# K and Q leave PSUM as one 128-row piece and reach their rows by DMA; their weights are split in the first stage and kept in DRAM

## The chip, the cores and the metric

The kernel runs on one core of a Trainium2 chip. Its time is device microseconds (us) of one execution. The engines are called PE (TensorE, the matrix unit, with PEld for its weight loads), DVE (VectorE), ACT (ScalarE), POOL (GpSimd) and SP (SyncE, which here only issues DMAs). Each takes its instructions in the order of its own queue and waits on semaphores for the others. DMAs are issued from SP's queue and from POOL's.

## The reference

Two layers on x (1024 tokens of width 1024, float32). Layer 0 is a gated mixer and a SwiGLU feed-forward of width 2816. Then K and V are made once from the stream, and layer 1 is a differential attention with its own queries, and a second feed-forward.

```python
kv = rms_norm(x, g) @ w_kv                       # K: 8 heads x 2 maps x 64, V: 8 heads x 128
q = (h @ w_q).reshape(B, S, N_HEADS, 2, HEAD_DIM)
...
s = einsum(q, k) * scale + bias                  # ALiBi bias, causal
p = softmax(s)
a = p[:, :, 0] - lam * p[:, :, 1]                # the two maps of a head
o = rms_norm(a @ v, subln) * (1 - lambda_init)
x = x + o.reshape(B, S, V_WIDTH) @ w_o
x = x + swiglu(rms_norm(x, ffn_norm), w_gu, w_down)
```

## The kernel before

The activations lie transposed: width on the 128 partitions, tokens along the rows, in two halves of 512. Every float32 operand of a product is split into a high part (a cast by ACT) and a low part (the rest, a subtraction by DVE), and three products, high x high, high x low and low x high, replace one. `split` is that pair of instructions.

The stages follow each other: the mixer's projections z and u, its spatial gate and the product with w_out (0 to about 395 us, the entry to the first feed-forward included); the first feed-forward (up to about 982 us, its down product from about 735 us); the projection of V, whose result goes to DRAM (`vscr`); the attention, eight heads (1096 to 1482 us); the second feed-forward and the final norm.

In the mixer, `post_z` and `post_u` take each finished product tile out of PSUM: `post_u` multiplies by a row scale on DVE, applies a gelu on ACT, and multiplies into z on POOL. Behind them `more`, sums of the pieces of w_out and of z, is made by POOL for the output product.

In the attention a generator, `proj_stream`, makes K and Q of the next head while the scores of the present one run. It yields between product steps, and the loop over the blocks of a head calls it, so that PE's projection products fill its waits. A head has four parts: K and Q for each half of the tokens. A part is 24 products into one PSUM tile of 128 rows, and rows 0 to 63 belong to the first of the two maps, rows 64 to 127 to the second. The scores take K and Q as operands of 128 rows in which the map's 64 rows of the high part stand beside 64 rows with the low part (K), or with a second copy (Q). Before, for each map, ACT writes the high part of 64 rows and DVE the low part of the 64 rows into place (L1163 to L1167), and for Q a DMA on POOL's queue copies 64 rows to the other 64 (L1169); in the last head ACT and DVE write those too. `get_w` fetches the weights of a head's K or Q with `Pieces`: a load on SP's queue (L184), a multiplication by the norm's gain on POOL (L201), and a split (L163 on ACT, L164 on DVE).

The order of the instructions on an engine is the order in which a list scheduler places them; at the transitions between stages a few orders are written out by hand (`T.order`). The sums of squares for a norm are `acc` (class `Norm`): ACT squares, POOL adds, and DVE adds the last part; PE then sums over the partitions (`dn<-mean,acc`) and spreads the result over rows (`dn<-ident,nr`). In the down products `cut` is a split operand, and L674 forms differences of weight blocks for an algorithm with fewer products.

## Time and profile before

| | us |
|---|---|
| median of 3 runs | 2207.34 |
| lowest and highest run | 2204.45, 2210.29 |
| the profiled execution's own time | 2203.82 |
| its span, first to last instruction | 2202.1 |

The span is a little shorter than the time of the execution, as the time holds what lies around the first and the last instruction. A row of the trace has the start, the duration, the engine, the line, and what the instruction writes and reads (`out<-in`); a bracket behind it gives the time for which the engine stood idle before it, and the instruction that released it.

### The profile page before, as it was taken

What the parts mean: (1) busy time and instruction counts of PE and PEld (TensorE: products, weight loads), DVE (VectorE), ACT (ScalarE), POOL (GpSimd) and SP (SyncE); (2) the same over time, 40 slices, a digit from 0 to 9 for tenths busy, and PEclk for the clock granted to TensorE, in tenths of its full rate; (3) what the DMA queues carried; (4) which work ended last, traced back from release to release, by engine and by line L of the source; (5) the groups of instructions that cost most, each with busy time, mean ns of one, the idle gap of its engine ahead of it and who ended that gap; (6) DMA issues with size and microseconds to landing.
All of it is one profiled execution on the core that took longest, in us unless ns stands there. A gap on an engine that the chain in (4) does not pass through costs nothing.

```text
span 2202.1 us, 30208 instructions
## 1 busy us (share of the span) xinstructions
PE 2118.6 (96%) x10640; PEld 1771.6 (80%) x10640; DVE 1442.2 (65%) x2541; ACT 1217.1 (55%) x2436; POOL 980.5 (45%) x856
## 2 busy tenths in 40 slices
PE   9999888999999989999999999999799999999998
PEld 7888666888888868878788888887588888888887
DVE  5545997544545576775288898865955454547685
ACT  5323455666666534453277777743467676654463
POOL 5023668675766400244123323205876767560024
PEclk9999999999999999999999999999999999999999
DMA  4131111222223774235423334573123232259412
GB/s 163 58 105 66 40 58 72 98 109 101 106 91 120 244 257 158 77 111 161 117 73 91 87 89 122 187 260 118 63 82 115 101 111 101 96 176 355 132 52 105
DMA packets 111321, 265.85 MB, mean 121 GB/s; under 512 B 10401, under 2 KB 20641, under 8 KB 104257
## 3 DMA queue, kind: packets, MB, share of 16 engines
q1 hardware_dynamic: 93808, 224.98, 29.3%
q0 software_dynamic: 17360, 38.93, 6.3%
q8 instruction: 84, 1.38, 0.3%
q14 instruction: 69, 0.56, 0.1%
HBM read 179.47 MB, written 77.07 MB: 116 GB/s over the span
## 4 chain that ended last, share of the span: by engine, by line
PE 78%; DVE 11%; DMA 4%; POOL 3%; issue 2%; ACT 2%; SPq 0%; DVEq 0%; ACTq 0%; POOLq 0%
PE mm L39 54%; PE d L39 15%; PE sc L39 3%; PE po L39 2%; PE tr L42 2%; DVE cut L646 1%; DVE wg L164 1%; DMA w<-in_w_down 1%; DVE w_lo L164 1%; DVE w_hi L164 1%; DMA a<-ascr 1%; DVE E L1242 1%; PE tr L39 1%; DVE x L160 1%; DVE E L1254 1%
## 5 line engine op out<-in xcount | busy, mean ns | idle before, releaser
L39 PE MATMUL d<-cut 128*128 128x512 f32 (+1 forms) x1788 | 407.7, 388 | 15.7 <-ACT cut L645 9.8
L39 PEld LDWEIGHTS d<-cut 128*128 128x128 f32 x1788 | 332.6, 189 | 88.0 <-ACT cut L645 10.8
L462 DVE TENSOR_TENSOR c<-c,mm 128x256 f32<-128x256 f32 (+1 forms) x300 | 151.2, 506 | 179.5 <-PE mm L39 162.0
L137 POOL TENSOR_TENSOR acc<-acc,sq 128x512 f32<-128x512 f32 (+1 forms) x64 | 92.6, 1449 | 378.3 <-ACT sq L133 376.4
L309 DVE TENSOR_TENSOR wg<-row,wg 128x512 fp32r<-128x512 f32 x180 | 116.7, 658 | 94.6 <-ACT wg L308 90.9
L39 PE MATMUL mm<-hT_hi,w_hi 128*128 128x512 f32 x384 | 155.9, 406 | 0.0
L39 PE MATMUL mm<-hT_hi,w_lo 128*128 128x512 f32 x384 | 151.5, 394 | 0.0
L39 PE MATMUL mm<-hT_lo,w_hi 128*128 128x512 f32 x384 | 150.9, 393 | 0.0
L645 ACT CAST cut<-a 128x512 fp32r<-128x512 f32 x110 | 68.1, 620 | 146.4 <-PE d L39 140.5
L39 PE MATMUL mm<-fine,wg 128*128 128x256 f32 x960 | 138.5, 285 | 4.4 <-DVE c L462 3.5
L39 PEld LDWEIGHTS mm<-fine,wg 128*128 128x128 f32 x960 | 130.5, 191 | 14.0 <-ACT wg L308 3.9
L321 ACT COPY c<-mm 128x512 f32<-128x512 f32 x152 | 88.9, 585 | 91.3 <-PE mm L39 50.8
L646 DVE TENSOR_TENSOR cut<-a,cut 128x512 fp32r<-128x512 f32 x110 | 89.2, 811 | 75.0 <-ACT cut L645 74.9
L308 ACT CAST wg<-S 128x512 fp32r<-128x512 f32 x160 | 99.2, 620 | 50.0 <-PE mm L39 49.3
L331 POOL TENSOR_TENSOR S<-graw 128x512 f32<-128x512 f32 x44 | 59.5, 1352 | 147.6 <-DMA graw<-in_w_gu 147.6
L39 PE MATMUL mm<-T1h,wg 128*128 128x512 f32 x352 | 116.8, 393 | 4.8 <-DVE wg L309 2.3
L39 PE MATMUL mm<-T2h,wg 128*128 128x512 f32 x352 | 118.0, 397 | 1.4 <-ACT wg L308 0.9
L39 PE MATMUL mm<-B22h,wg 128*128 128x512 f32 x352 | 117.5, 396 | 1.0 <-DVE wg L164 0.7
L39 PE MATMUL mm<-B11h,wg 128*128 128x512 f32 x352 | 117.7, 395 | 0.5 <-DVE wg L309 0.5
L39 PE MATMUL mm<-T3h,wg 128*128 128x512 f32 x352 | 118.0, 397 | 0.0
L1246 ACT ACTIVATE E<-E,nm 128x256 f32<-128x256 f32 (+7 forms) x128 | 99.5, 778 | 33.2 <-DVE nm L1242 31.5
L341 POOL TENSOR_TENSOR c<-c,c 128x512 f32<-128x512 f32 x80 | 103.5, 1304 | 31.0 <-DVE c L462 31.0
(287 smaller groups left out, 5784.2 us busy)
## 6 DMA issues: line engine op xcount, KB each, us to landing
graw<-in_w_gu SPq DMA_DIRECT2D x44, 1024.0 KB, 4.9
ascr<-c SPq DMA_DIRECT2D x154, 256.0 KB, 2.0
a<-ascr SPq DMA_DIRECT2D x12, 1280.0 KB, 6.4
a<-ascr SPq DMA_DIRECT2D x18, 768.0 KB, 4.9
xscr<-x SPq DMA_DIRECT2D x48, 256.0 KB, 2.1
w<-in_w_down SPq DMA_DIRECT2D x14, 768.0 KB, 10.6
a0b<-ascr SPq DMA_DIRECT2D x12, 768.0 KB, 5.2
x<-xscr SPq DMA_DIRECT2D x16, 512.0 KB, 12.1
```

Of the source, the lines that this page charges most:

```text
L39: return self._keep(self.engine.matmul(*args, **kw))
L137: return (V if last else G).tensor_tensor(self.acc, self.acc, part, op=ALU.add)
L164: return V.tensor_tensor(lo, src, hi.bitcast(F32), op=ALU.subtract)
L308: A.copy(w[:, 0], src)
L309: T.note(line, name, V.tensor_tensor(w[:, 1], near, w[:, 0].bitcast(F32), op=ALU.subtract))
L321: A.copy(r, src)
L331: T.note(line, ("S1", layer, j, gu), G.tensor_tensor(s1, a21, a22, op=ALU.add))
L341: (G if j else V).tensor_tensor(g, g, u, op=ALU.mult)
L462: V.tensor_tensor(c, c, ps, op=ALU.add)
L645: A.copy(o[:, 0], src)
L646: T.note(line, name + ("lo",), V.tensor_tensor(o[:, 1], src, o[:, 0].bitcast(F32), op=ALU.subtract))
L1246: A.activation(Em[:, :L], Em[:, :L], AF.Exp, scale=-1.0, bias=nm, accum_out=acc)
```

## The change

Four things. (1) A part of K or Q leaves PSUM with one ACT and one DVE instruction of 128x512 into a new tile `both`; four DMAs on POOL's queue bring its halves to their rows, for K 128 KB each and for Q 256 KB each. The last head does the same as the others. (2) The weights of K and Q are multiplied by the gain and split in the first stage: `split_weights` makes 16 pieces, one for each call of `next(ahead)` in `post_z` and `post_u`, and stores high and low part to DRAM (`wscr`). Its tiles come from a pool with one buffer. (3) `get_w` loads the two parts from there, by two DMAs on POOL's queue. (4) The gains are loaded earlier, and the memory for the descriptors of POOL's DMAs is set to 4096 bytes.

```diff
+    wscr = tc.dram_tile([2 * H, P, 2, 1024], F32R, name="wscr")
...
+        prep = pool(front, "pre")
...
+        kvg = col(kv_norm, KD, "kvg")
+        bg = col(b_norm, KD, "bg")
+
+        def split_weights():
+
+            for i in range(2 * H):
+                raw = prep.tile([P, KD, P], F32, name="raw")
+                nc.sync.dma_start(out=raw, in_=(w_k, w_q)[i % 2][i // 2].rearrange("p (k c) -> p k c", c=P))
+                G.tensor_tensor(raw, raw, (kvg, bg)[i % 2].unsqueeze(2).broadcast_to([P, KD, P]), op=ALU.mult)
+                both = prep.tile([P, 2, 1024], F32R, name="both")
+                split(both[:, 0], both[:, 1], raw.rearrange("p k c -> p (k c)"))
+                nc.sync.dma_start(out=wscr[i].bitcast(F32), in_=both.bitcast(F32))
+                yield
+
+        ahead = split_weights()
...
             if cb:
+                next(ahead, None)
                 st6 = sm.tile([P, 2, 6], F32, name="st6")
...
             G.tensor_tensor(z[h][:, :, gs], z[h][:, :, gs], u.rearrange("p (j c) -> p j c", c=P), op=ALU.mult)
+            next(ahead, None)
...
                         q = [qp.tile([P, 2, 512], F32R, name=f"Q{m}") for m in range(2)] if kind else None
+                        both = kp_.tile([P, 2, 512], F32R, name="both")
+                        if kind:
+                            A.activation(both[:, 0], ps, AF.Copy, scale=0.125)
+                            V.scalar_tensor_tensor(both[:, 1], ps, 0.125, both[:, 0].bitcast(F32), ALU.mult, ALU.subtract)
+                        else:
+                            split(both[:, 0], both[:, 1], ps)
                         for m in range(2):
                             own, oth = slice(m * 64, m * 64 + 64), slice(64 - m * 64, 128 - m * 64)
-                            if not kind:
-                                A.copy(K[m][own, hs], ps[own])
-                                V.tensor_tensor(K[m][oth, hs], ps[own], K[m][own, hs].bitcast(F32), op=ALU.subtract)
-                            else:
-                                A.activation(q[m][own, 0], ps[own], AF.Copy, scale=0.125)
-                                V.scalar_tensor_tensor(q[m][own, 1], ps[own], 0.125, q[m][own, 0].bitcast(F32), ALU.mult, ALU.subtract)
-                                if h < H - 1:
-                                    G.dma_start(out=q[m][oth], in_=q[m][own])
+                            for i, to in enumerate((own, oth)):
+                                if kind:
+                                    G.dma_start(out=q[m][to], in_=both[own])
                                 else:
-                                    A.activation(q[m][oth, 0], ps[own], AF.Copy, scale=0.125)
-                                    V.scalar_tensor_tensor(q[m][oth, 1], ps[own], 0.125, q[m][own, 0].bitcast(F32), ALU.mult, ALU.subtract)
+                                    G.dma_start(out=K[m][to, hs], in_=both[own, i])
...
-                    src, g = ((w_k, kvg), (w_q, bg))[kind]
                     with tc.issue_after(marks["spill"]):
-                        weights[h, kind] = piece(src[h], g)
+                        w = [wq_p.tile([P, 1024], F32R, name=n) for n in ("w_hi", "w_lo")]
+                        for i in range(2):
+                            G.dma_start(out=w[i], in_=wscr[2 * h + kind, :, i])
+                        weights[h, kind] = w
...
-    nc = bacc.Bacc("TRN2", target_bir_lowering=False, num_devices=1)
+    nc = bacc.Bacc("TRN2", target_bir_lowering=False, num_devices=1, dynamic_dma_scratch_size=4096)
```

The edits move instructions at places that they don't touch, too. The lines of the changed kernel have other numbers: L164 is the same, L682 is L681 of before, L647 is L646, L675 is L674, L988 is L970 and L1048 is L1029.

The first place is POOL's order at the end of the mixer, where L907 is the new multiplication of a weight by its gain, `z<-z,u` the last multiplication of `post_u`, and `more` a sum for the output product. In the changed kernel:

```order
L988 TENSOR_TENSOR z<-z,u 128x4x128 x2
L907 TENSOR_TENSOR raw<-raw,bg 128x1024
L907 TENSOR_TENSOR raw<-raw,kvg 128x1024
L988 TENSOR_TENSOR z<-z,u 128x4x128
L1048 TENSOR_TENSOR more<-wo_1790 128x512 x4
L988 TENSOR_TENSOR z<-z,u 128x4x128 x2
L907 TENSOR_TENSOR raw<-raw,bg 128x1024
L988 TENSOR_TENSOR z<-z,u 128x4x128
L1048 TENSOR_TENSOR more<-z 128x512 x4
```

The three L907 are new, the last of them stands ahead of the last z; the others stand as before.

The second place is DVE's order between the first feed-forward's last sums (`x<-x,d`) and the projection of V (`vt` is the low part of a tile of V, `w_lo` that of its weights, L146 the first step of the norm behind PE's means). Before:

```order
L197 SCALAR_TENSOR_TENSOR w_lo<-raw,kvg,w_hi 128x512 x4
L681 TENSOR_TENSOR x<-x,d 128x512 x4
L137 TENSOR_TENSOR acc<-acc,sq 128x512
L197 SCALAR_TENSOR_TENSOR w_lo<-raw,kvg,w_hi 128x512 x2
L146 TENSOR_SCALAR nm_8354<-dn 128x4
L164 TENSOR_TENSOR vt<-mm,vt 128x4x128
```

And in the changed kernel:

```order
L682 TENSOR_TENSOR x<-x,d 128x512 x4
L164 TENSOR_TENSOR vt<-mm,vt 128x4x128
L197 SCALAR_TENSOR_TENSOR w_lo<-raw,kvg,w_hi 128x512
L137 TENSOR_TENSOR acc<-acc,sq 128x512
L197 SCALAR_TENSOR_TENSOR w_lo<-raw,kvg,w_hi 128x512 x3
L146 TENSOR_SCALAR nm_8475<-dn 128x4
```

The first `vt` and one `w_lo` moved ahead of `acc`. On ACT the cast of that `vt` now stands ahead of four `w_hi`, before it stood behind two of them; on POOL five loads of K and Q weights stand ahead of the last `acc` addition there.

The third place is DVE's order at the start of the last down product. Before:

```order
L646 TENSOR_TENSOR cut<-a_18709,cut 128x512
L646 TENSOR_TENSOR cut<-w_18707,cut 128x512
L646 TENSOR_TENSOR cut<-a_18709,cut 128x512
L674 TENSOR_TENSOR w_18707<-w_18712,w_18707 128x512 x4
L646 TENSOR_TENSOR cut<-w_18707,cut 128x512
L646 TENSOR_TENSOR cut<-a0b,cut 128x512
```

And in the changed kernel:

```order
L675 TENSOR_TENSOR w_18836<-w_18841,w_18836 128x512 x3
L647 TENSOR_TENSOR cut<-a_18838,cut 128x512
L647 TENSOR_TENSOR cut<-w_18836,cut 128x512
L647 TENSOR_TENSOR cut<-a_18838,cut 128x512
L647 TENSOR_TENSOR cut<-w_18836,cut 128x512
L647 TENSOR_TENSOR cut<-a0b,cut 128x512
```

Three of the differences moved ahead of the cuts. On SP's queue one load of `a0b` (768 KB) that stood ahead of the `w` loads now stands further ahead, between loads of `w2b`.

## Rows read from the trace of the kernel before

**Rows 1.** The page's busy times: engine, us, share of the span, instructions.

```profile
PE 2118.6 (96%) x10640; PEld 1771.6 (80%) x10640; DVE 1442.2 (65%) x2541; ACT 1217.1 (55%) x2436; POOL 980.5 (45%) x856
```

**Rows 2.** Windows of the mixer: stretch, its length, then busy time (instructions) by engine.

```profile
core 0: us, PE busy (x) PEld busy (x) DVE busy (x) ACT busy (x) POOL busy (x), PEclk, DMA share, GB/s
150.00:200.00 50.00, 50.00 (x240) 41.65 (x239) 26.57 (x37) 14.85 (x22) 11.39 (x8) 1.00 0.25 95
200.00:250.00 50.00, 43.50 (x184) 33.65 (x182) 41.43 (x43) 20.83 (x38) 33.51 (x22) 0.97 0.17 63
```

**Rows 3.** Windows of the attention, columns as in rows 2.

```profile
1050.00:1450.00 400.00, 394.09 (x2194) 337.70 (x2193) 320.07 (x858) 259.91 (x686) 106.45 (x114) 1.00 0.40 118
1150.00:1200.00 50.00, 49.49 (x287) 42.67 (x287) 44.75 (x122) 36.97 (x99) 14.83 (x15) 1.00 0.30 85
```

**Rows 4.** PE's waits in six heads, 1120 to 1392 us: in total, times, longest.

```profile
PE tr L42 <- DVE E L1254: 2.6, 6, 0.4
```

**Rows 5.** The timeline around one such wait.

```profile
1164.90 1.89 POOL L201 TENSOR_TENSOR raw<-raw,kvg 128x1024 f32<-128x1024 f32 x1
...
1165.28 1.53 DVE L1253 SCALAR_TENSOR_TENSOR cc<-s,nlam,s 128x1 f32<-128x1 f32 x1
...
1168.01 0.84 PE L42 MATMUL tr<-ident,E 128*128 128x128 f32 x6 [0.42 <-DVE E L1254]
```

**Rows 6.** Groups by shape, 1120 to 1392 us: busy us, mean ns, idle before.

```profile
L164 DVE TENSOR_TENSOR w_lo<-raw,w_hi 128x1024 fp32r<-128x1024 f32 x13 | 16.9, 1301 | 0.0
...
L1164 DVE TENSOR_TENSOR K<-mm,K 64x512 fp32r<-64x512 f32 x24 | 16.5, 689 | 2.1 <-ACT K L1163 1.5
...
L201 POOL TENSOR_TENSOR raw<-raw,bg 128x1024 f32<-128x1024 f32 x6 | 13.5, 2254 | 11.2 <-DMA raw<-in_w_q 11.2
...
L1169 POOL DMA_DIRECT2D Q<-Q x22 | 11.5, 522 | 42.5 <-DVE Q L1167 21.0 <-issue 9.9 <-PE tr L42 8.2
```

**Rows 7.** DMA issues, 1120 to 1392 us: KB each, median us to landing.

```profile
Q<-Q POOLq DMA_DIRECT2D x22, 256.0 KB, 3.2
...
raw<-in_w_q SPq DMA_DIRECT2D x6, 512.0 KB, 3.7
```

**Rows 8.** POOL's timeline early in the mixer.

```profile
34.29 2.65 POOL L137 TENSOR_TENSOR acc<-acc,sq 128x512 f32<-128x512 f32 x2
```

**Rows 9.** The timeline at the end of the mixer.

```profile
217.03 1.29 POOL L970 TENSOR_TENSOR z<-z,u 128x512 f32<-128x512 f32 x1 [0.21 <-ACT u L969]
...
230.40 1.75 DVE L164 TENSOR_TENSOR w_hi<-z,w_hi 128x512 fp32r<-128x512 f32 x1
232.07 0.68 DVE L164 TENSOR_TENSOR w_lo<-wo,w_lo 128x512 fp32r<-128x512 f32 x1
```

**Rows 10.** The timeline ahead of the V projection.

```profile
983.77 0.69 DVE L137 TENSOR_TENSOR acc<-acc,sq 128x512 f32<-128x512 f32 x1 [1.18 <-ACT sq L133]
987.15 0.95 PE L39 MATMUL dn<-mean,acc 128*128 128x1 f32 x8
987.22 1.34 ACT L196 ACTIVATE w_hi<-raw,kvg 128x512 fp32r<-128x512 f32 x2 [3.91 <-DMA raw<-in_w_v]
987.98 1.42 DVE L197 SCALAR_TENSOR_TENSOR w_lo<-raw,kvg,w_hi 128x512 fp32r<-128x512 f32 x2 [3.52 <-ACT w_hi L196]
988.47 0.56 ACT L163 CAST vt<-mm 128x512 fp32r<-128x512 f32 x1
```

**Rows 11.** Windows of 4 us in the mixer's output product, columns as in rows 2.

```profile
236.00:240.00 4.00, 1.22 (x5) 0.79 (x5) 4.00 (x6) 1.34 (x3) 0.88 (x1) 1.00 0.12 47
240.00:244.00 4.00, 3.90 (x10) 2.86 (x11) 4.00 (x5) 2.12 (x4) 2.89 (x2) 0.57 0.56 215
```

**Rows 12.** The timeline at the start of the last down product.

```profile
1977.27 11.00 PE L39 MATMUL d<-cut 128*128 128x512 f32 x47
1977.46 0.94 SPq L600 DMA_DIRECT2D w<-in_w_down  x2
...
1985.88 2.50 DVE L674 TENSOR_TENSOR w<-w,w 128x512 f32<-128x512 f32 x4 [0.90 <-DMA w<-in_w_down]
...
1989.03 3.24 PE L39 MATMUL d<-cut 128*128 128x512 f32 x13 [0.77 <-DVE cut L646]
```

More of the change, by code (lines that the diff above doesn't have):

```diff
@@ L1083, in trunk @@
         wq_p = right(mid, "wqk", 4)
-        kvg = col(kv_norm, KD, "kvg")
-        bg = col(b_norm, KD, "bg")
         with ExitStack() as att:
```

## The prediction

> **What bounds the kernel now.** I read the busy times first, then the windows of the two stages that change, then the waits of TensorE (PE) in them, then single stretches in time order. PE works for 2118.6 us [rows 1] of a span of 2202.1 us, so all its idle time together is 83.5 us, and a change can win only what of that lies where it works. It works in two places. In the first stage PE is busy for 50.00 us of the 50 from 150 to 200, with VectorE (DVE) at 26.6 and GpSimd (POOL) at 11.4; from about 205 us, where the gate's last pieces go into the output product, PE falls to 43.5 of 50 and DVE rises to 41.4 [rows 2]. A filler on DVE or POOL is free before 205 us and is paid for behind it. The other place is the attention (about 1096 to 1482 us). DVE is busy 44.75 us of 50 there, which looks like a bound, but PE is at 49.49, and in the 400 us from 1050 on it stands idle for 400 - 394.09 = 5.9 us in all [rows 3]: PE sets the time.
>
> What PE waits for there is told by its waits: 2.6 us in six heads, each time a transpose behind a DVE instruction [rows 4]. One of the six, step by step: POOL multiplies a K weight by its gain for 1.89 us, beside it DVE's tiny `cc`, 128x1, takes 1.53 us, the E behind it comes late, and PE's transposes start 0.42 us late [rows 5]. Six times 0.42 is the 2.6 us. The reader should see that a job of 1.9 us on an engine off the path costs PE 0.4 us by way of DVE.
>
> **The attention.** Each head loses two weight splits on DVE (1.30 us each) and four of the eight subtractions of 64x512 (0.69 us each), since an instruction on 128 partitions does in one what two on 64 did. That is 2 x 1.30 + 4 x 0.69 = 5.4 us of DVE in a head of 45.3 us (six in the 272 us of that view), and two POOL multiplies of up to 2.25 us [rows 6]. None of it is on PE; PE gets back its waits. The 2.6 us go with the multiply beside `cc`; 5.9 us is all its idle time. I take **-4.0**, in the middle, bounds -2.6 and -5.9.
>
> What is added here stands on POOL's queue: 16 transfers for K and Q in a head in place of four, and four loads of weights. With 0.52 us for an issue [rows 6], 16 more are 8.3 us, against 4.1 us of multiplies. POOL's 14.8 us of 50 are 13.4 in a head [rows 3]; they become about 17.6. The bias and r stand behind the new issues, and PE's scores wait for DVE, which waits for those; both have some 27 us of POOL's idle time in a head. K and Q are read only by the next head's scores, so a landing of 3.2 us [rows 7] is hidden. Price nothing, while issues stay near 0.52 us.
>
> One rule of the notes belongs to the row with `cc`. The Trainium skill ("SBUF — State Buffer", section "SBUF: two separate sides") says that DVE and GpSimd hold a common port pair by an exclusive lock, and that the loser blocks for the whole instruction. The trace agrees in kind: 1.53 us for a 128x1 instruction. By the rule the two multiplies of a head could stop DVE for 4.1 us, 25 us in six heads; but DVE is not the bound, and the sum by PE's waits stays at -4.
>
> **The split moved to the front.** Each of 16 steps is a load on SP (3.7 us, as w_q's now [rows 7]), a POOL multiply (1.9 to 2.25 us), an ACT cast and a DVE subtraction (1.30 us) [rows 6], and a store. The step's tiles have one buffer, so the steps stand one behind another, at 9 to 11 us each: 3.7 + 2.25 + 1.30, about 1.1 for ACT (estimated from DVE's), and 1 to 3 us of waiting in the queues. The first multiply stands in POOL's order among the sums of squares at 34 to 38 us [rows 8]. The sixteenth would then be ready at 38 + 15 x (9 to 11) = 173 to 203 us. All together this is 21 us on DVE and 34 us on POOL over 165 us, in which DVE has 23 of 50 us free and POOL 38 [rows 2], while PE is full; a late post is caught by the four PSUM buffers of the products. So the first fifteen cost nothing. Without this cover, every us that a post is late beyond those buffers would be PE's: rival 2.
>
> The sixteenth cannot come when it is ready: in POOL's order it stands behind the four `more` and before the last z product, which starts at 217.03 us, while DVE sets the time [rows 9]. A multiply there puts z and the next `more` off by 2.25 us, DVE's own share of the step is 1.3 us, and beside a POOL instruction DVE's 128x512 pieces take 1.75 instead of 0.68 us [rows 9], 1.1 us for one. Of these 4.65 us about half falls in DVE's and POOL's gaps: **+2.5**, bounds 0 and 5.
>
> **The junction before the V projection.** DVE's sum of squares `acc` starts at 983.77 us, and PE takes its mean products at 987.15 without a wait [rows 10]. After, DVE's `vt` of the first V tile and one w_lo stand ahead of `acc`. `vt` needs PE's whole first tile, which ends where the mean products begin, then ACT's cast (0.56 us); the w_lo needs an ACT w_hi behind that cast (0.67 us) and takes 0.71 us itself; `acc` takes 0.69 us [rows 10]. So `acc` is there at 987.3 + 0.56 + 0.67 + 0.71 + 0.69 = 989.9 us, and the mean products, whose place on PE is unchanged, wait 2.7 us. With the queues' delays **+3**, bounds 2 and 6. The upper bound has two sources: POOL's last part of the same sum now stands behind five loads of weights, and the clock. Behind a window in which PE worked 1.22 us of 4, the granted clock of the next was 0.57, about the lower of the two levels, 1.2 of 2.4 GHz [rows 11]; at that rate 4 us of work lose 1.7 us.
>
> **The second transition, into the last down product.** DVE's differences of w (2.50 us for four) wait for a load issued at 1977.46 us and start at 1985.88; ahead of them it makes three cuts, and PE runs 47 products from 1977.27 to 1988.27 and waits 0.77 us [rows 12]. After, three of the differences stand ahead of those cuts. PE wants the first of the pairs 12 products before the end of the 47, at 1988.27 - 12 x 0.234 = 1985.5 us; it would be there at 1985.88 + 3 x 0.62 + two cuts at about 0.65 = 1989.0 us. PE waits 3.5 us there and no longer the 0.77: +2.7. If the load lands 2 us earlier, since a load of 768 KB leaves its place ahead of it, +0.7. I take **+2**, bounds 0 and 5.
>
> The products of both FFNs from 238 to 940 and from 1520 to 1950 us keep their order on all engines: zero.
>
> **Sum.** -4 + 2.5 + 3 + 2 = +3.5 us. The profiled execution took 2203.82 us; with 3.5 it is 2207.3. The median of the three runs, 2207.34 us, stands 3.5 above that execution, so on the median it is **2211 us**, 0.16% more.
>
> **The rivals.** (1) Faster: the attention gives back all 5.9 us and the two transitions cost nothing, because the DVE instructions moved ahead find their operands early. 2207.3 - 5.9 = 2201.4 us. That both wait for something which the trace shows late (the first tile's end, the load) speaks against it. To be faster by more than 0.3% (6.6 us, about what a measurement can tell from no change) it needs some of PE's idle time elsewhere too.
>
> (2) Slower, by the front's queues. SP and POOL take their instructions in order: a load that lands late holds the multiply, the multiply holds each z product behind it, and the loads of w_u stand on SP behind the stores. The point that decides is the length of a step: the sixteenth multiply keeps its place as long as a step takes under (217 - 38) / 15 = 11.9 us. At 12.5 us it is ready at 225.5, and the output product slides by 8.5 us: 2211 + 8.5 = 2219.5 us. For it speaks that I could only estimate the waiting; against it, that DMA and POOL are nearly idle there.
>
> (3) Slower, by POOL's queue in the attention. Of its 13.4 us in a head, 4.1 go and 2.1 are the four old issues, so 7.2 us remain; POOL fills a head of 45.3 us when 20 issues take (45.3 - 7.2) / 20 = 1.9 us each. From there each further 0.1 us costs 2 us a head, 14 us in seven heads: 2225 us. A mean of 0.52 us over 22 issues [rows 6] speaks against it. The Trainium skill ("DMA: Bandwidth & Descriptors", section "SWDGE vs HWDGE vs iDMA") is for it: plain transfers belong to SP or ACT, and DVE can lock GpSimd out while it writes descriptors. The 22 issues beside a DVE at 44.75 of 50 us do not show this.
>
> (4) The aim is missed, because PE is full: -2.6 us in the attention, and the transitions cost nothing. 2204.7 us.
>
> **How the numbers follow.** Forecast 0.50, with a range of its own of 2205 to 2217 (the terms at their bounds do not all fall on one side); rival 1 0.13, rival 2 0.15, rival 3 0.07, rival 4 0.15. The range reaches from rival 1 to past rival 2, 2200 to 2222 us; rival 3 and the tails stay out. Slower than 2214 us: rivals 2 and 3 and a quarter of the forecast, 0.34. Faster than 2200.7 us: most of rival 1, 0.10. Within 0.3%: the rest, 0.56.
>
> **What the profile after would show.** Attention: heads shorter by 0.4 to 0.6 us, no wait of a transpose for E, DVE near 39 of 50, issues near 0.52 us. Front: no idle PE before 205 us, and the last multiply near 217. Junction: a wait of PE's mean products for `acc`, some 3 us. Second transition: a wait for a cut, some 3 us. The prediction is wrong if PE idles before 205 us, if POOL fills up in the attention, or if the two waits are absent.

## The result, and the profile after

The changed kernel takes 2225.48 us (median of five runs, 2221.72 to 2233.34), the kernel before on the same chip 2204.45 us. The ratio is 1.0093, interval 1.0077 to 1.0109: 21 us slower, where I had forecast 3.5 us. The profiled execution took 2233.34 us, the longest of the five.

PE has 15 us more of busy time than in [rows 1] for the same 10640 instructions, so a part of the loss is work at a lower clock and not waiting: the mean granted clock of the profiled execution is 0.981, before the change 0.989. DVE and ACT have less, POOL has 132 instructions more. This is the page's row of busy times:

```profile
PE 2133.8 (96%) x10640; PEld 1784.4 (80%) x10640; DVE 1420.1 (64%) x2505; ACT 1190.4 (53%) x2400; POOL 1047.8 (47%) x988
```

Every kernel here gives PE the same number of products. So I read, at the borders of a stage, how much later the product with the same number starts than in the profile of before; what the difference grows by in a stage is that stage's loss. In the changed kernel it is +3.3 us at the end of the mixer (205 to 260 us of before's time), +9.6 at the junction ahead of V (980 to 1020), -5.4 in the heads of the attention (1020 to 1396), +7.4 in the last head (1396 to 1475) and +3.7 at the second transition (1972 to 1995). These five make 18.6 us of the 29.5 by which the two spans (2202.1 and 2231.6 us) differ. The other 11 us lie mostly at 280 to 300 us (+2.4), 700 to 850 us (+2.6) and in the tail, 2150 to 2195 us (+4.8). At the first and the last of these a second profile of the kernel before differs from its first one as well (last section); at 700 to 850 us it does so by only 0.4 us, but e12 below, which has every instruction of the changed kernel in the same order, loses 0.2 us there. The medians are only 21 us apart.

**Attention.** First a window that answers to the second of [rows 3], then six heads of 45.3 us of before's length (columns as in [rows 2]). DVE has 38.24 us of 50 instead of 44.75, POOL 20.88 instead of 14.83, and PE 49.91 instead of 49.49:

```profile
1167.00:1217.00 50.00, 49.91 (x295) 43.75 (x294) 38.24 (x118) 31.02 (x93) 20.88 (x33) 1.00 0.65 164
1135.00:1407.00 272.00, 271.46 (x1587) 237.37 (x1586) 207.31 (x625) 170.50 (x499) 112.46 (x171) 1.00 0.67 168
```

The groups by shape in those six heads show an issue at 0.53 us (0.52 in [rows 6]), and `cc` at 0.22 us on the mean and at most. Before, most took 0.22 us too, but six of them took over 1.5 us, as the one in [rows 5]. Of the six waits of [rows 4] none is left:

```profile
L1189 POOL DMA_DIRECT2D K<-both x48 | 25.2, 533 | 32.6 <-ACT both L163 23.4 <-DVE both L164 7.7 <-issue 1.1
L1187 POOL DMA_DIRECT2D Q<-both x47 | 24.4, 535 | 23.0 <-DVE both L1180 20.4 <-DMA oa<-oscr 1.3 <-DMA w_hi<-wscr 0.9
L1272 DVE SCALAR_TENSOR_TENSOR cc<-s,nlam,s 128x1 f32<-128x1 f32 x49 | 10.7, 218 | 1.1
```

**Junction.** PE's waits from 980 to 1010 us are one row, and [rows 10] had none:

```profile
PE dn L39 <- DVE acc L137: 6.0, 1, 6.0
```

The timeline shows what DVE's `acc` stood behind. SP issues the loads of w_v at 990.75 us. ACT needs the first at 998.73 and has stood idle for 3.09 us for it; DVE's w_lo comes behind it, `acc` behind the w_lo:

```profile
990.75 0.87 SPq L184 DMA_DIRECT2D raw<-in_w_v  x2
...
995.68 0.69 DVE L164 TENSOR_TENSOR vt<-mm,vt 128x512 fp32r<-128x512 f32 x1 [5.37 <-ACT vt L163]
...
998.73 1.33 ACT L196 ACTIVATE w_hi<-raw,kvg 128x512 fp32r<-128x512 f32 x2 [3.09 <-DMA raw<-in_w_v]
999.49 0.75 DVE L197 SCALAR_TENSOR_TENSOR w_lo<-raw,kvg,w_hi 128x512 fp32r<-128x512 f32 x1 [3.12 <-ACT w_hi L196]
1000.16 0.68 DVE L137 TENSOR_TENSOR acc<-acc,sq 128x512 f32<-128x512 f32 x1
```

Why the load is late stands in the table of DMA issues from 985 to 1000 us. Eight loads of the new weights, 4 MB, were put into the same stretch by POOL's queue (from 989.54 us), and w_v takes 9.0 us to land; the loads of w_v ahead of the junction took 4.8 before the change (last line, its table from 975 to 992 us):

```profile
w_hi<-wscr POOLq DMA_DIRECT2D x4, 512.0 KB, 10.4
w_lo<-wscr POOLq DMA_DIRECT2D x4, 512.0 KB, 10.6
...
raw<-in_w_v SPq DMA_DIRECT2D x2, 512.0 KB, 9.0
```

```profile
raw<-in_w_v SPq DMA_DIRECT2D x4, 512.0 KB, 4.8
```

The windows (columns as in [rows 2]) show the other part. PE works 0.02 us of 5, and behind that the granted clock is 0.50, the lower of the two levels, and then 0.67. At those rates 4.01 and 5.00 us of work lose 2.0 and 1.7 us. With the wait of 6.0 that is 9.7, against the 9.6 read at the borders:

```profile
995.00:1000.00 5.00, 0.02 (x1) 0.00 (x0) 1.21 (x2) 1.85 (x3) 1.08 (x2) 0.81 1.07 390
1000.00:1005.00 5.00, 4.01 (x14) 3.56 (x15) 2.99 (x6) 1.40 (x3) 1.04 (x1) 0.50 1.12 416
1005.00:1010.00 5.00, 5.00 (x19) 3.96 (x18) 1.23 (x3) 0.51 (x1) 0.00 (x0) 0.67 1.14 396
```

**Last head.** Two waits from 1400 to 1450 us carry most of the loss; PE's waits there make 5.1 us, and at the same place before the change 1.7:

```profile
PE po L39 <- DVE on L1301: 2.4, 1, 2.4
PE tr L42 <- DVE E L1273: 2.2, 1, 2.2
```

Both go back to a load again. The output product's weights w_o land 13.4 us after their issue. In the same stretch are the last twelve of the last head's sixteen K and Q transfers and the loads of `oa`, the attention's output read back for that product (4 MB). Before the change w_o took 5.2 us (second table, 1395 to 1432 us in each profile):

```profile
oa<-oscr POOLq DMA_DIRECT2D x8, 512.0 KB, 8.1
Q<-both POOLq DMA_DIRECT2D x8, 256.0 KB, 10.8
...
raw<-in_w_o SPq DMA_DIRECT2D x2, 512.0 KB, 13.4
...
K<-both POOLq DMA_DIRECT2D x4, 128.0 KB, 11.0
```

```profile
raw<-in_w_o SPq DMA_DIRECT2D x2, 512.0 KB, 5.2
```

ACT stands for each of the two loads, and what PE wants of ACT and DVE stands in their order behind the casts (timeline of ACT):

```profile
1424.66 1.04 ACT L163 CAST w_hi<-raw 128x1024 fp32r<-128x1024 f32 x1 [3.15 <-DMA raw<-in_w_o]
...
1430.85 1.05 ACT L163 CAST w_hi<-raw 128x1024 fp32r<-128x1024 f32 x1 [3.62 <-DMA raw<-in_w_o]
```

From 1425 to 1440 us the granted clock is below full in three windows of 5 us, where it was 1.00 before the change, and that makes most of the rest:

```profile
1425.00:1430.00 5.00, 2.44 (x11) 2.16 (x11) 3.18 (x8) 2.23 (x6) 0.00 (x0) 0.82 1.26 250
1430.00:1435.00 5.00, 2.83 (x15) 2.52 (x14) 2.70 (x8) 3.02 (x11) 0.00 (x0) 0.84 0.43 147
1435.00:1440.00 5.00, 5.00 (x17) 4.03 (x16) 2.32 (x8) 2.39 (x10) 1.04 (x1) 0.66 0.52 184
```

**Front.** The first, the ninth and the last two multiplies of the split on POOL (timeline). From the first to the sixteenth are 181.6 us, 12.1 a step:

```profile
37.30 1.91 POOL L907 TENSOR_TENSOR raw<-raw,kvg 128x1024 f32<-128x1024 f32 x1
...
129.84 1.90 POOL L907 TENSOR_TENSOR raw<-raw,kvg 128x1024 f32<-128x1024 f32 x1 [8.63 <-DVE vl L164]
...
206.00 1.90 POOL L907 TENSOR_TENSOR raw<-raw,kvg 128x1024 f32<-128x1024 f32 x1 [8.59 <-DMA raw<-in_w_k]
218.86 1.89 POOL L907 TENSOR_TENSOR raw<-raw,bg 128x1024 f32<-128x1024 f32 x1
```

From 35 to 205 us PE does not idle. From 200 to 245 us it works 36.79 us, and before the change 38.50 (windows of the two kernels).

**Second transition.** The row of PE's waits, and DVE's timeline, which answers to [rows 12]: three differences stand ahead of the cuts, behind the load.

```profile
PE d L39 <- DVE cut L647: 2.8, 1, 2.8
```

```profile
2005.81 1.90 DVE L675 TENSOR_TENSOR w<-w,w 128x512 f32<-128x512 f32 x3 [5.91 <-DMA w<-in_w_down]
2007.63 0.68 DVE L647 TENSOR_TENSOR cut<-a,cut 128x512 fp32r<-128x512 f32 x1
```

### The profile page after: what moved, and what is told of

It is laid out like the page before. It is cut to its first block, busy times and chain, and to the rows that moved or that the text cites. A ratio compares the mean times of both kernels' runs of the same rounds, so it can differ in the third digit from the quotient of the medians.

```text
span 2231.6 us, 30438 instructions
## 1 busy us (share of the span) xinstructions
PE 2133.8 (96%) x10640; PEld 1784.4 (80%) x10640; DVE 1420.1 (64%) x2505; ACT 1190.4 (53%) x2400; POOL 1047.8 (47%) x988
## 4 chain that ended last, share of the span: by engine, by line
PE 79%; DVE 10%; DMA 4%; POOL 3%; ACT 2%; issue 2%; SPq 0%; DVEq 0%; ACTq 0%; POOLq 0%
PE mm L39 54%; PE d L39 16%; PE sc L39 3%; PE po L39 3%; PE tr L42 2%; DVE cut L647 1%; DVE wg L164 1%; DMA w<-in_w_down 1%; DVE w_lo L164 1%; DVE w_hi L164 1%; PE tr L39 1%; DMA raw<-in_w_o 1%; DMA a<-ascr 1%; DMA raw<-in_w_v 1%; DVE x L160 1%
## 5 line engine op out<-in xcount | busy, mean ns | idle before, releaser
L39 PE MATMUL d<-cut 128*128 128x512 f32 (+1 forms) x1788 | 409.2, 389 | 18.7 <-ACT cut L646 9.4
L646 ACT CAST cut<-a 128x512 fp32r<-128x512 f32 x110 | 68.2, 620 | 148.4 <-PE d L39 141.8
L647 DVE TENSOR_TENSOR cut<-a,cut 128x512 fp32r<-128x512 f32 x110 | 90.2, 821 | 71.9 <-ACT cut L646 71.8
```

The costliest lines, as they stand in the source:

```text
L39: return self._keep(self.engine.matmul(*args, **kw))
L646: A.copy(o[:, 0], src)
L647: T.note(line, name + ("lo",), V.tensor_tensor(o[:, 1], src, o[:, 0].bitcast(F32), op=ALU.subtract))
```

## The experiments

The table has the ratio to the kernel before on the same chip, and what each profile lost (+) or won at the five places, in us, read as above. e0 is the kernel before, profiled once more: what it loses no change has caused. The column "tail" is 2150 to 2195 us.

| kernel | ratio (95%) | front | junction | attention | last head | 2nd trans. | tail |
|---|---|---|---|---|---|---|---|
| changed | 1.0093 (1.0077, 1.0109) | +3.3 | +9.6 | -5.4 | +7.4 | +3.7 | +4.8 |
| e0 before again | one run | 0.0 | 0.0 | 0.0 | -0.1 | +0.6 | +3.7 |
| e1 K/Q only | 1.0030 (1.0019, 1.0041) | 0.0 | 0.0 | -3.4 | +1.1 | +5.3 | 0.0 |
| e2 weights only | 1.0063 (1.0050, 1.0076) | +3.3 | +8.7 | -4.3 | 0.0 | +3.3 | +3.6 |
| e5 loads later | 1.0083 (1.0068, 1.0098) | +3.3 | +7.5 | -5.4 | +6.0 | +4.1 | +4.8 |
| e9 acc first | 1.0068 (1.0045, 1.0092) | +3.3 | +6.7 | -5.4 | +2.0 | +2.2 | +4.8 |
| e10 loads spread | 1.0042 (1.0024, 1.0059) | +3.3 | 0.0 | -5.3 | +0.3 | +4.1 | +3.6 |
| e4 last head old | 1.0071 (1.0044, 1.0097) | +3.3 | +8.8 | -4.7 | 0.0 | +4.4 | +3.6 |
| e8 eight steps | 1.0065 (1.0041, 1.0088) | -1.1 | +8.6 | -5.3 | +1.9 | +3.6 | +4.7 |
| e12 (no effect) | 1.0075 (1.0060, 1.0090) | +3.3 | +8.5 | -5.4 | +2.3 | +3.8 | +3.6 |
| e15 cut first | 1.0069 (1.0049, 1.0089) | +3.3 | +8.9 | -5.4 | +7.6 | -1.0 | +3.7 |
| e11 three repairs | 1.0008 (0.9996, 1.0019) | -0.6 | 0.0 | -3.6 | 0.0 | +3.4 | +3.6 |
| e16 four repairs | 0.9994 (0.9983, 1.0005) | -0.6 | 0.0 | -3.6 | 0.0 | -1.0 | +4.8 |
| e14 K/Q, one repair | 1.0007 (0.9992, 1.0022) | -1.1 | 0.0 | -2.8 | -0.1 | +4.1 | +4.8 |
| e17 K/Q, two repairs | 0.9980 (0.9969, 0.9992) | -1.1 | 0.0 | -2.8 | 0.0 | -1.0 | +3.6 |

The columns do not add up to a kernel's time. Read in the same way, 280 to 300 us, 700 to 850 us and the entry to the second feed-forward (1490 to 1520 us) differ from profile to profile, the last from -0.6 to +4.6 us: there the changed kernel has +1.0 and e12, in the same order, +3.9. The larger memory for descriptors and the earlier loads of the gains are in every kernel of the table but e0, and no run measures them alone; e17 has both and is not slower.

### The two halves of the change: e1, e2

e1 is the changed kernel with the weights as before, without `split_weights`:

```diff
-                        w = [wq_p.tile([P, 1024], F32R, name=n) for n in ("w_hi", "w_lo")]
-                        for i in range(2):
-                            G.dma_start(out=w[i], in_=wscr[2 * h + kind, :, i])
-                        weights[h, kind] = w
+                        weights[h, kind] = piece(src[h], g)
```

e2 has the new weights and the old copies of K and Q:

```diff
-                        both = kp_.tile([P, 2, 512], F32R, name="both")
...
+                            if not kind:
+                                A.copy(K[m][own, hs], ps[own])
+                                V.tensor_tensor(K[m][oth, hs], ps[own], K[m][own, hs].bitcast(F32), op=ALU.subtract)
```

> The changed kernel with its weights as before (load, multiply and split in the attention, nothing in the first stage): only K and Q leave PSUM in one piece. Theory A (three prices at three places: the split in the first stage 6.6 us, the 4 MB of weight loads at the V projection 9.6 us, the transfers of K and Q in the last head 7 us): the first two are gone, the waits of the transposes for E stay as the multiplies stay, so it ends about 5 us above the kernel before, some 2209 us, and PE idles about 5 us or more around the last head. Theory B (the transfers of K and Q fill POOL's queue and the DMA engines through the whole attention and cost most of the 21 us): about 2220 us. Theory C (the prices come from the moved weights alone): 2200 to 2204 us, and no wait in the last head.

> The changed kernel with K and Q written by ACT and DVE to their rows as before: only the weights are split in the first stage and loaded from DRAM. Theory A: the first stage (+6.6) and the V projection (+9.6) cost as in the changed kernel, the heads shorten by about 0.5 us each, the last head is as before; 2204.5 + 6.6 + 9.6 - 3 = about 2217 us. Theory B: near the kernel before, 2204 to 2208 us. Theory C: the whole loss, 2225 us.

Theory A foresaw 5 us for e1 and 13 us for e2; their medians are 7.5 and 14.4 us above that of the kernel before. It put e1's last head at 7 us, which cost 1.1, and left out the second transition, which cost 5.3. Both halves are slower, and the ratios add up to that of the change (0.30% and 0.63%, against 0.93%). Each wins most of the attention by itself, 3.4 and 4.3 us; together they win 5.4, since PE has hardly any idle time left there to give back (0.5 us in the six heads). Front and junction belong to the weights. The last head's large loss is in neither alone. The second transition is in both, though e1 touches nothing near it: what moves there is the order that the scheduler gives DVE.

### The junction: e5, e9, e10

e5 lets the loads of the weights start later, e9 sets DVE's `acc` ahead of the `vt` and the w_lo, e10 spreads the loads of heads 0 and 1 over the tiles of V.

e5, in `get_w`:

```diff
-                    with tc.issue_after(marks["spill"]):
+                    with tc.issue_after(marks["pow"]):
```

e9, in the projection of V:

```diff
+                T.order({0: line["acc", 0, 0, 3] + line["vt", 0, 0]}, [0])
+                T.order({0: line["acc", 0, 0, 3] + line["down", 0, 1, "mean"] + line["vlo", 5]}, [0])
```

e10, in `get_w`, where `marks["vt", ...]` is the store of a V tile:

```diff
-                    with tc.issue_after(marks["spill"]):
+                    with tc.issue_after(marks["vt", h, (2, 5)[kind]] if h < 2 else marks["spill"]):
```

> The changed kernel with the first eight loads of weights from DRAM issued behind the norm ahead of the V projection; DVE's order there falls back to that of before by itself. Theory A (the loads of V's weights landed late, behind 4 MB of other loads, and DVE's sum of squares stood behind one of them): PE's wait of 6.0 us for that sum goes, and the granted clock does not fall there; 9 us less than the changed kernel, about 2216 us. Rival (the sum is late because it stands behind the first V tile on DVE, and the loads do not matter): the same here, as the order changes too, so this run tells only whether the junction carries 9 us; the next one tells which.

> The changed kernel with its eight loads where they are, but on DVE the sum of squares stands ahead of the first V tile, and it and the first step of the norm stand ahead of the four low parts of V's weights that the late loads feed. Theory A1 (the late loads cost only through DVE's order): PE's wait of 6.0 us goes, as with the later loads, about 2216 us, although the loads of V's weights still take 8 us. Theory A2 (PE itself needs what is late, or POOL's five loads ahead of its part of the sum hold it up): the wait moves to another place between 995 and 1010 us and 5 us or more stay, about 2222 us.

> The changed kernel with the first four pairs of weight loads spread over the projection of V, one pair behind the stores of tiles 2, 5, 10 and 13; DVE's order at the junction falls back to that of before. Theory A2 (4 MB at once is what costs, and the wait moves to what lands late wherever they are put together): no wait over 1 us from 985 to 1100 us, 9 us less than the changed kernel, about 2216 us. Rival (the loads themselves, wherever they are, hold up V's stores and PE): PE waits again for the low parts of V's tiles, 2 us or more at each pair.

In e5 and e9 the wait for `acc` is gone, and another stands there, so the 9 us that e5 was to win did not come. e5, PE's waits from 980 to 1035 us: `acc` is first again and w_v lands in 4.4 us, but now the stores of V stand in the same heap of transfers. ACT stands idle for 12.35 us for one of them before it casts the next V tile, and PE waits behind that:

```profile
PE mm L39 <- DVE vt L164: 5.7, 1, 5.7
```

e9, DVE's timeline: `acc` is there at 990.85 us, but the norm's eight multiplications of x start behind the last late w_lo, at 1000.39, and the `vt` that PE waits for (3.9 us) comes at 1007.58:

```profile
990.85 0.69 DVE L137 TENSOR_TENSOR acc<-acc,sq 128x512 f32<-128x512 f32 x1 [3.52 <-POOL acc L137]
...
1000.39 4.86 DVE L810 TENSOR_TENSOR x<-x,dn 128x512 f32<-128x512 f32 x8
...
1007.58 0.68 DVE L164 TENSOR_TENSOR vt<-mm,vt 128x512 fp32r<-128x512 f32 x1
```

In e10 nothing waits there; w_v lands in 4.3 us, and the order that I had priced does not occur: DVE makes `acc` first. The kernel is at 2214.92 us, as theory A2 had it (2216):

```profile
989.37 0.69 DVE L137 TENSOR_TENSOR acc<-acc,sq 128x512 f32<-128x512 f32 x1 [0.83 <-ACT sq L133]
993.71 1.42 DVE L197 SCALAR_TENSOR_TENSOR w_lo<-raw,kvg,w_hi 128x512 fp32r<-128x512 f32 x2 [3.65 <-ACT w_hi L196]
```

So the 4 MB in one place are the cause: with them three different orders lose 9.6 (changed), 7.5 (e5) and 6.7 us (e9), and without them the order of before loses nothing. Since e10 changed both, what the new order alone would have cost is not measured. In the changed kernel 3.09 us of the wait of 6.0 are ACT's standing for w_v; the other 2.9 would be the order's, an estimate from these two rows.

### The last head: e4

e4 gives the last head alone its copies by ACT and DVE back.

```diff
+                        if h == H - 1:
+                            for m in range(2):
+                                own, oth = slice(m * 64, m * 64 + 64), slice(64 - m * 64, 128 - m * 64)
+                                if not kind:
+                                    A.copy(K[m][own, hs], ps[own])
...
+                        else:
                             both = kp_.tile([P, 2, 512], F32R, name="both")
```

> The changed kernel with K and Q of the last head alone written by ACT and DVE as before. Theory A (the transfers of K and Q meet the 4 MB of oa loads, and the load of w_o, which ACT waits for, lands after 13 us instead of 5): the load lands after 5 to 6 us, the 7.4 us in the last head go, about 2218 us. Rival (the 4 MB of oa loads and the w_o load meet badly by themselves, as the heads are shorter): the load still takes over 10 us, 2223 us or more.

The loss there is 0.0, and w_o lands in 4.6 us (DMA issues, 1395 to 1432 us):

```profile
oa<-oscr POOLq DMA_DIRECT2D x4, 512.0 KB, 8.8
...
raw<-in_w_o SPq DMA_DIRECT2D x2, 512.0 KB, 4.6
```

So theory A holds at the place. The ratio, 1.0071, is below the changed kernel's 1.0093 but not clear of the 1.0075 that the same kernel has as e12.

In the kernels whose last head has its K and Q by DMA, w_o's median landing goes with the loss: 9.6 us and +0.3 (e10), 10.5 and +1.1 (e1), 10.5 and +1.9 (e8), 10.8 and +2.0 (e9), 11.1 and +2.3 (e12), 12.5 and +6.0 (e5), 13.4 and +7.4 (changed), 13.6 and +7.6 (e15). e12 and the changed kernel issue the same instructions in the same order, so with nothing else changed the last head costs 2.3 or 7.4 us as the transfers happen to meet.

### The front: e8

e8 makes eight of the sixteen pieces; heads 4 to 7 read the weights of heads 0 to 3.

```diff
-            for i in range(2 * H):
+            for i in range(H):
...
-                            G.dma_start(out=w[i], in_=wscr[2 * h + kind, :, i])
+                            G.dma_start(out=w[i], in_=wscr[(2 * h + kind) % H, :, i])
```

> The changed kernel with eight of the sixteen steps of the split in the first stage; heads 4 to 7 read the weights of heads 0 to 3. Theory A (only the last step, at 218 us, costs): the 6.6 us that PE has lost by 300 us are gone but for what the clock does there, 0 to 4 us stay; 2219 to 2222 us. Rival (the steps cost by their number): half, 3.3 us, stay and about 2222 us. Where between the two readings overlap, the waits of PE from 205 to 300 us decide: with A no step's instruction stands there.

The last multiply is at 116.23 us, and the front wins 1.1 us where it had lost 3.3, so the rival (half of the loss stays) is out. With twelve steps (e11, e16) the loss is gone too: it is that of the last four, whose multiplies stand from 182.21 to 218.86 us. Whether they cost by coming late or by their place in POOL's order, no run separates.

### The second transition: e12, e15

The added order sets the three cuts on DVE ahead of the differences. In e12, and in e11 and e14, the line stood behind its loop and changed no order; e12 is the changed kernel measured a second time.

```diff
                         s = V.tensor_tensor(to[i], x[i], y[i], op=ALU.subtract)
                         T.order({0: [line[name + ("lo",)][2 * i + 1], s.ins]}, [0])
+                        if layer and name[2] == 0 and i < 4:
+                            T.order({0: [line[name + ("lo",)][8], s.ins]}, [0])
```

> The changed kernel with one thing alone: in the second transition DVE makes the cut that PE waits for ahead of the first difference of w, as before the change. Theory A (the order of DVE's instructions is the cause there): PE's wait for that cut goes from 2.8 us to under 1, the difference to the kernel before at that place from +3.7 to under +1, all else as in the changed kernel; time 2222 us, ratio 1.0080. Rival B (the load that the differences wait for is what is late): PE's wait stays at 2 to 3 us, now for the differences, and the time stays at the changed kernel's 2225 us.

> The changed kernel with one thing alone, now in force: in the second transition DVE makes three cuts ahead of the first four differences of w, as before the change. Theory A: PE's wait for a cut falls from 2.8 us to under 1, the difference to the kernel before at that place from +3.7 to under +1; ratio 0.0013 under that of the changed kernel (1.0093 and, in a second measurement, 1.0075), so 1.0062 to 1.008. Rival B: the wait stays at 2 us or more for a cut behind the differences, the ratio where it was.

In e15 PE waits for nothing there, and instead of 3.7 us lost the place wins 1.0: theory A, the order. The ratio, 1.0069, is in A's range, but not clear of e12's 1.0075; the place decides. DVE's timeline has the three cuts ahead of the four differences:

```profile
2002.04 0.88 DVE L647 TENSOR_TENSOR cut<-a,cut 128x512 fp32r<-128x512 f32 x1 [3.89 <-ACT cut L646]
2002.84 0.68 DVE L647 TENSOR_TENSOR cut<-w,cut 128x512 fp32r<-128x512 f32 x1
2003.44 0.68 DVE L647 TENSOR_TENSOR cut<-a,cut 128x512 fp32r<-128x512 f32 x1
2004.04 2.48 DVE L675 TENSOR_TENSOR w<-w,w 128x512 f32<-128x512 f32 x4
```

### All repaired: e11, e16, e14, e17

e11 is e10 with e4's last head and only twelve steps in the front (heads 6 and 7 take their weights as before the change); e16 adds the order of e15. e14 is e1 with e4's last head; e17 adds the order. Beside the edits above, e11 and e16 have:

```diff
-            for i in range(2 * H):
+            for i in range(2 * H - 4):
...
+                if H - 2 <= h < H and (h, kind) not in weights:
+                    src, g = ((w_k, kvg), (w_q, bg))[kind]
```

> Four repairs of the changed kernel together: the loads of heads 0 and 1 are spread over the V tiles, the last head's K and Q are copied by ACT and DVE as before the change, only twelve of the sixteen weights are split in the first stage (heads 6 and 7 get theirs in the attention, as before the change), and DVE makes its cut ahead of the differences of w in the second transition. Theory A (four losses, each with a cause of its own and each removed by its own repair; the attention's gain stays): PE's differences to the kernel before are about 0 at 205 to 260 us, 0 at 980 to 1020, -4.5 in the attention, 0 in the last head, +0.5 at the second transition; time 0.2% under the kernel before, 2199 to 2202 us if that is at 2204.5. Rival B (what one place wins, another gives back, by transfers that land together or by the clock): one of the four places keeps 3 us or more, or a new one appears, and the time is no better than with spread loads alone, ratio 1.004, 2213 us. Rival C (time of the stretches that hold the same work, as at 280 to 300 us and in the tail, comes and goes by where the queues meet): places as in A, but the time 3 to 6 us above A's.

> The four repairs together, the fourth now in force: the loads of heads 0 and 1 spread over the V tiles, the last head's K and Q copied by ACT and DVE, twelve of the sixteen weights split in the first stage, and in the second transition the three cuts ahead of the first four differences of w. The same without the fourth measured 1.0008, with +3.4 us at the second transition. Theory A (that place's loss comes from DVE's order alone): the wait goes to under 1 us, the difference there to under 1, and the time is 0.10 to 0.15% under that: ratio 0.9985 to 1.0, 2204 to 2207 us beside a kernel before at 2207. Rival B (the load that the differences wait for is late): DVE's next cuts, now behind the differences, make PE wait 2 us or more; ratio 1.0005 to 1.001.

> K and Q leave PSUM in one piece in all heads but the last, the weights as before the change, and the cut ahead of the differences in the second transition. Theory A (copying in one piece wins 3.4 us in the attention and loses only at the last head and the second transition): -3.4 in the attention, 0 elsewhere, ratio 0.9985 to 0.9995, 2201 to 2203.5 us if the kernel before is at 2204.5. Rival B (the extra transfers cost something in other places too, as the ratio 1.003 of the same edit without the repairs would say if the last head's 1 us and the transition's 5 us were not all): ratio over 1.001, 2207 us or more.

> K and Q leave PSUM in one piece in all heads but the last, the weights as before the change, and the three cuts ahead of the differences in the second transition, now in force. The same without that order measured 1.0007, with +4.1 us at the second transition and -2.7 in the attention. Theory A: the transition's loss falls under 1 us, ratio 0.9985 to 0.9995, 2204 to 2206 us beside a kernel before at 2207. Rival B: the wait moves to a later cut, ratio 1.0003 to 1.001.

e11 and e14 missed what theory A foresaw for them (ratios of 0.998 and at most 0.9995): they are at 1.0008 and 1.0007. Both still lose at the second transition, +3.4 and +4.1 us, where their order had no effect. e16 and e17 lose at none of the five places, and in the attention they win 3.6 and 2.8 us.

e17 measures 2203.48 us against 2208.63, ratio 0.9980 (0.9969, 0.9992), so it is some 0.2% faster. Not all of it belongs to K and Q in one piece. That is worth 2.8 us in the attention. The 1.0 us at the transition is the written order's, which the kernel before could have as well (not run). The 1.1 us in the front are not tied to the edit: e1 issues the same instructions there in the same order and has 0.0.

The whole change repaired, e16, comes out between: 0.9994 (0.9983, 1.0005). Its attention is 0.8 us better than e17's. It loses 3.4 us from 700 to 850 us, where e17 wins 0.7, and wins 2.2 us from 1475 to 1972 us, where e17 loses 3.5; so the profiles do not show why its median is the higher one. e11 and e12 do not lose from 700 to 850 us and the changed kernel loses 2.6, so that is again not tied to one edit. The two intervals overlap, and whether the new weights are worth anything beside e17 stays open.

## Why the prediction was wrong

By its steps, for the profiled execution:

- **Attention**, -4 with bounds -2.6 and -5.9: -5.4. PE's waits for E are gone in the six heads, DVE stands at 38.2 of 50 (I had said near 39), an issue takes 0.53 us, POOL works 112.46 / 6 = 18.7 us a head (17.6). Right, near the bound that is all of PE's idle time.
- **Front**, +2.5 with bounds 0 and 5: +3.3. No idle PE from 35 to 205 us, and the sixteenth multiply at 218.86 (I had said near 217). A step took 12.1 us, not 9 to 11, and so 0.2 over the 11.9 from which rival 2 was to begin. So rival 2's mechanism did begin, but the sixteenth came only 1.9 us late, and the place cost 3.3 us, where rival 2 had 8.5 at 12.5 us a step.
- **Second transition**, +2 with bounds 0 and 5: +3.7. The wait is 2.8 us, and the granted clock behind it is 0.84 and 0.82 in windows of 5 us. The order of DVE is the cause, as e15 shows.
- **Junction**, +3 with bounds 2 and 6: +9.6. This is the first step that failed. The wait for `acc` is in the right place, but its price was worked out from DVE's and ACT's durations alone, on the operands being there. w_v's landing took 4.2 us longer than before, and ACT, which makes the w_lo's operand from it, stood idle for 3.09 us; the wait became 6.0 us where 2.7 had been worked out. I had counted the loads of weights on POOL's queue only as issues ahead of POOL's part of the sum; that part was done at 993.76 us and cost nothing. The loss at the lower clock, which I had put at 1.7 us as an upper bound, was 3.7.
- **Last head**, nothing: +7.4. The second step that failed, and the sentence is "K and Q are read only by the next head's scores, so a landing of 3.2 us [rows 7] is hidden. Price nothing, while issues stay near 0.52 us." Issues did stay there, and PE indeed waits for neither K nor Q. But in the last head twelve of their transfers meet the `oa` and w_o loads, and w_o, which had taken 5.2 us, took 13.4, and PE's waits and the lower clock behind it make most of the 7.4 us. The size is partly chance: e12, with the same instructions in the same order, lost 2.3 us there.

The two that failed are one mistake: a transfer was priced by the time of its issue on the queue and by who waits for it, not by what else is in flight. The Trainium skill ("DMA: Bandwidth & Descriptors", section "Issuing engines are not separate DMA queues") says that transfers of all issuing engines run on the same 16 engines and interleave; the landings of SP's w_v and w_o behind POOL's transfers agree, at 9.0 for 4.8 and 13.4 for 5.2 us.

Set against the sum, junction (+6.6), last head (+7.4), transition (+1.7), front (+0.8) and attention (-1.4) are 15.1 us more than foreseen. The profiled execution is 26.0 us above the sum's 2207.3; the remaining 11 are those of 280 to 300 us, 700 to 850 us and the tail, which the section on the result could not tie to the change. The median is 14.5 us above the 2211. None of the three signs that the prediction named for being wrong came: PE did not idle from 35 to 205 us, POOL did not fill up, and both waits were there. It had no sign for a wait of the right kind and the wrong size, nor for the last head. Rival 3 (POOL's queue full) is refuted: it needed 1.9 us an issue, and at DVE's 38.2 of 50 us the rows show 0.53.

## What to carry to other kernels

Price a moved or added DMA by what is in flight beside it: list the loads that land with little to spare in that stretch, and ask which engine's order stands behind each. Megabytes that may come at any time are issued in small lots between stores that are already there, not at one mark. Where a list scheduler orders the engines, a win in one stage can be lost to a new order in a stage that the change doesn't touch, so pin the orders at the transitions before the change is judged.

## What was not expected of the hardware

The kernel before, profiled twice with the same instructions in the same order, differs by 3.7 us in its tail. DVE's cuts of 128x512 and POOL's additions of the same size meet there, and the two profiles show two ways in which that goes. In the first profile (timeline from 2161 us) POOL's addition takes 4.80 us, and DVE's cuts keep their 0.69:

```profile
2166.05 0.69 DVE L646 TENSOR_TENSOR cut<-a,cut 128x512 fp32r<-128x512 f32 x1
2166.10 4.80 POOL L807 TENSOR_TENSOR x<-x,near 128x512 f32<-128x512 f32 x1
...
2168.46 0.69 DVE L646 TENSOR_TENSOR cut<-a,cut 128x512 fp32r<-128x512 f32 x1
```

In the second (e0) POOL's three take 1.70 us each and DVE's cuts up to 1.77; PE waits 3.2 us in all for them and for `kept`, DVE's other low parts of this product:

```profile
2175.32 5.11 POOL L807 TENSOR_TENSOR x<-x,near 128x512 f32<-128x512 f32 x3
2175.83 1.77 DVE L646 TENSOR_TENSOR cut<-a,cut 128x512 fp32r<-128x512 f32 x1
2177.53 1.76 DVE L646 TENSOR_TENSOR cut<-w,cut 128x512 fp32r<-128x512 f32 x1
```

By the tail's column, all profiles but that of e1 went the second way, so the first profile was the rarer case, and a loss read against it alone would have been put down to the change. The Trainium skill ("SBUF — State Buffer", section "SBUF: two separate sides") tells of a pair of ports that DVE and GpSimd hold in turn for a whole instruction; both profiles agree with that, and none of the runs shows what decides who waits.

At 280 to 300 us, too, profiles of kernels that do the same there lie between 0 (e17) and +4.1 us (e1); e0 stands at +1.6, and from 284 to 292 us its granted clock is 0.78 and 0.80, where the first profile of before has 1.00 throughout.
